# A two-layer trunk with four token mixers and a mixture of experts: the first layer's experts in groups of four with 96 slots each, norm1 without GpSimd, rows replicated on the host, and another instruction order

## The chip, the cores and the metric

One NeuronCore of a Trainium2 chip runs the whole program; the other cores are idle. The metric is device time in microseconds of one execution. The profile names the engines PE (TensorE matmul), PEld (TensorE weight load), DVE (VectorE), ACT (ScalarE), POOL (GpSimd) and SP (SyncE, which here only issues DMAs); PEclk is the granted TensorE clock as a share of the higher of its two levels (1.2 and 2.4 GHz).

## The reference, cut to what matters

```python
D_MODEL, SEQ, DEPTH, CTX_LEN = 1024, 256, 2, 256
N_EXPERTS, TOP_K, D_EXPERT = 16, 2, 256
def adaln(cond, w_mod, b_mod):
    m = jax.nn.silu(cond) @ w_mod + b_mod          # w_mod 1024 x 6144
    return jnp.split(m[..., None, :], N_MOD, axis=-1)
def trunk_layer(x, xc, ...):
    h = rms_norm(x, lp["norm1_g"]) * (1.0 + mod[1]) + mod[0]      # latent; hc for context likewise
    ... = jnp.split(h @ lp["w_in"], splits, axis=-1)              # w_in 1024 x 6544
    ya_l, yb_l, yc_l, yd_l = fourier, RWKV-7, DeltaNet, S5 mixers
    x = x + mod[2] * merge_branches((ya_l, yb_l, yc_l, yd_l), gate_l, lp["w_branch"], lp["w_out"])
    h2 = rms_norm(x, lp["norm2_g"]) * (1.0 + mod[4]) + mod[3]
    x = x + mod[5] * moe_ffn(h2, ...)
def moe_ffn(h, ...):                                # two experts of one group of four per token
    for e in range(N_EXPERTS):
        act = jax.nn.silu(h @ w1[e]) * (h @ w3[e])  # 1024 -> 256
        y = y + combine[..., e:e + 1] * (act @ w2[e])
```

Layer 0 computes 512 tokens (256 of context, 256 latent) and layer 1 needs only the 256 latent ones at its end. All is float32.

## The kernel before, in words

**Recording and order.** The kernel doesn't issue its instructions as it goes. Every operation is recorded, cut into some 1,480 units, and `nc.plan(RUNS)` goes over them: RUNS, a table of numbers, is the order of priority, and a cost model decides for each engine which ready operation comes next and which buffer it gets (43 buffers of 128 x 1024 words for weights, tokens and results, 8 PSUM banks). The program then holds one fixed order for each engine. SP issues most of the loads, ACT the small ones and the experts' result writes, POOL the gathers. A load takes one of eight semaphores in turn, shared by the loads of SP and of ACT, so an issue can wait for the load that had its semaphore before.

**Layer start.** `adaln` (before: matmul L1917, after: L1945) multiplies the two condition rows by w_mod, in rounds of 16 tiles `aw` of 512 KB; a matmul has 32 columns of weights, and four of them stand side by side in the array. `norm1_cols` (L1949) transposes the shift and scale of round 0. `norm1` (L1985) transposes the tokens with a diagonal matrix that holds 1/rms, and evicts each chunk of 128 x 256 as a high part `hT` (ACT, L1991) and a low part `hTl` (DVE L1992, then a subtraction at L1993 that alternates between DVE and POOL), so that the float32 input projection (`gemm`, L763) can run as products of two cheaper floats. The weights `cw` are split likewise (L639, L640).

**Mixers.** `s5_setup` builds the S5 branch's matrices from its parameters by many small matmuls (L1582 and L1606 to L1613) with DVE, ACT and POOL work between them. It doesn't depend on the tokens.

**Experts.** `moe` routes the tokens, writes them to DRAM (`h2d`), and takes the experts as blocks. In layer 0 a block is one expert with 128 slots: a gather of 128 token rows (`xg`), 8 transposes (L2115), 8 matmuls of 128 columns by 512 for w1 and w3 (`expert_up`, L2127), the activation (L2132 to L2134), 2 transposes (L2144), 4 matmuls by w2 (`expert_down`, L2154), and a write of the block's rows to DRAM (`ybd`). Each expert has 6 weight tiles `w` of 512 KB (L2092, L2096). Then each token gathers its two rows back (`yg`) and they are added with their weights (L2448 to L2450). In layer 1 a block is two experts with 64 slots, side by side in the array. A block of code under `tc.If(most > cap)` (L2401 to L2409) computes every expert for every token if an expert has more tokens than slots; with these inputs the largest expert has 96 tokens in layer 0 and 52 in layer 1.

```python
o1, ne = s5_setup(k, 1), NEXP + 2            # layer 1's S5 set-up is recorded among layer 0's experts
```

Of the kernel before, what the change touches and what calls it, by code (L numbers as in the profile page):

```python
# [24 lines left out]
NJ = 8  # L25
# [9 lines left out]
def host_consts():  # L35
# [18 lines left out]
    for k in c:  # L54
# [14 lines left out]
PACK = PRM + [("c", 16), ("norm1_g", 8), ("norm2_g", 8), ("s5_lam", 32), ("s5_log_step", 16), ("dn_ab", 16),  # L69
              ("router_w", 128), ("router_b", 16)]  # L70
# [6 lines left out]
def host_layout(a):  # L77
# [4 lines left out]
    for L in range(2):  # L82
# [3 lines left out]
        for n in ("norm1_g", "norm2_g"):  # L86
            p[n] = a[n][L].reshape(8, 128).T
# [110 lines left out]
def cost(o):  # L198
# [4 lines left out]
    if "dma" in o.name:  # L203
        return (0, 440, 0, 1000, 375)[o.eng], 0, math.prod(out.shape) * 4
    if o.eng == 0:
        if o.name == "transpose":
            return int(.85 * max(size(o.args[1]), size(o.args[2]))), 210, 0
        m, n = size(o.kw["lhsT"]), size(o.kw["rhs"])
        if o.kw["rhs"].dtype == F32:
            d = 2 * max(.85 * m + 4, .85 * n)  # L210
        else:
            d = max(.85 * m, .45 * n + 8)
        return int(d), 210, 0
    n = max([size(x) for a in list(o.args) + list(o.kw.values()) for x in aps(a)])
    if o.eng == 1:
        return int(50 + .9 * n), 160, 0
# [13 lines left out]
def part(o):  # L230
# [5 lines left out]
    n = len(rs) * len(cs)  # L236
    return sum(1 << (4 * x + y) for x in rs for y in cs), 100 if n > 8 else 50 if n > 4 else 35
# [27 lines left out]
class Tape:  # L265
    def __init__(self, tc, wk, ps):
# [6 lines left out]
        self.ops, self.tiles, self.spans, self.state, self.last_pe = [], {}, {}, {}, {}  # L273
# [17 lines left out]
    def access(self, ap):  # L291

        key = ap.tensor.name
        if key in self.tiles or ap.space != bass.MemoryType.DRAM:
            width = self.tiles[key].ap.shape[1] if key in self.tiles else NFIX
            c = (key in self.tiles, width, ap.offset, tuple(map(tuple, ap.ap)), ap.dtype)
# [8 lines left out]
    def add(self, eng, name, args, kw, reads=None, writes=None):  # L305
# [17 lines left out]
        for x, wr in [(r, False) for r in reads] + [(w, True) for w in writes]:  # L323
# [21 lines left out]
            else:  # L345
                st[1].append((op.pos, r0, r1, m))
            if eng == 0 and wr:
                o = self.last_pe.get(key)
                if o is not None:
                    op.pre.setdefault(o, 0)  # L350
                self.last_pe[key] = op.pos
# [11 lines left out]
    def plan(self, order=None):  # L363
# [23 lines left out]
        tiles.sort(key=lambda v: v.first)  # L387

# [25 lines left out]
        front, tab, wire, clock = 0, 0, 0, Clock()  # L414
        free, port = [0] * 6, [0] * 6
# [4 lines left out]
        for count in range(n):  # L420
# [30 lines left out]
            for v in new:  # L451
# [4 lines left out]
                if v.first > front:  # L456
                    held[v.kind][front:v.first] += 1
            d, f = o.dur, table(o)
            if f >= 0 and f != tab:
# [13 lines left out]
            if o.nbytes:  # L473
                wire = max(wire, t + d + 1300) + o.nbytes // 300
                o.end = wire + 500
# [320 lines left out]
def load_params(k, L):  # L796
# [3 lines left out]
    m = NPK - (144 if L else 0)  # L800
# [41 lines left out]
def rwkv(k, L, want_ctx):  # L842
# [180 lines left out]
    for s in range(8):  # L1023
# [69 lines left out]
    nc.scalar.dma_start(ln[:, 0], k.A["rw_ln_g"][L][None, :].to_broadcast([128, 256]))  # L1093
    nc.scalar.dma_start(ln[:, 1], k.A["rw_ln_b"][L][None, :].to_broadcast([128, 256]))
# [38 lines left out]
def deltanet(k, L, want_ctx):  # L1133
# [217 lines left out]
    for g in range(4):  # L1351
        p = psum(k, "dd")
        for u in range(8):
            for d in range(2):
                R = rows(d)
                nc.tensor.matmul(p[rows(1 - d), u * 64:u * 64 + 64], lhsT=KG[g // 2][R, g % 2 * 8 + u], rhs=ATu[R, g * 8 + u],
                                 start=True, stop=True, tile_position=(64 * d, 64 - 64 * d))
        for d in range(2):
            O = rows(1 - d)
            (nc.vector.tensor_copy if d else nc.scalar.copy)(hp2(WT[d][g // 2])[O, g % 2 * 512:g % 2 * 512 + 512], p[O])  # L1360
# [403 lines left out]
def fnet(k, L, want_ctx):  # L1764
# [808 lines left out]
```

## Time and profile before

| | us |
|---|---|
| time, median of 3 runs | 1659.14 (1657.5 to 1659.85) |
| time of the profiled execution | 1656.07 |
| its span | 1654.3 |
| PE busy in it | 1463.3 (88%) |
| PEld, DVE, ACT, POOL busy | 1031.0, 1054.4, 496.2, 359.1 |

The profiled execution lies 3.1 us under the median, and its time is 1.8 us longer than its span. Shares of the whole span hide that the stages have different limits, so the program is read here by stages: start 0 to 97 us (modulation, norm1), mixers and merge of layer 0 97 to 701, routing 701 to 768, experts of layer 0 768 to 983, combine and norm1 of layer 1 983 to 1033, mixers and merge of layer 1 1033 to 1490, routing 1490 to 1530, experts of layer 1 1530 to 1630, end 1630 to 1654.

### The profile page before, as it was taken

What the parts mean: (1) busy time and instruction counts of PE and PEld (TensorE: products, weight loads), DVE (VectorE), ACT (ScalarE), POOL (GpSimd) and SP (SyncE); (2) the same over time, 40 slices, a digit from 0 to 9 for tenths busy, and PEclk for the clock granted to TensorE, in tenths of its full rate; (3) what the DMA queues carried; (4) which work ended last, traced back from release to release, by engine and by line L of the source; (5) the groups of instructions that cost most, each with busy time, mean ns of one, the idle gap of its engine ahead of it and who ended that gap; (6) DMA issues with size and microseconds to landing.
All of it is one profiled execution on the core that took longest, in us unless ns stands there. A gap on an engine that the chain in (4) does not pass through costs nothing. (4 is left out here: it accounts for less than half of the span.)

```text
span 1654.3 us, 26410 instructions
## 1 busy us (share of the span) xinstructions
PE 1463.3 (88%) x10334; PEld 1031.0 (62%) x10334; DVE 1054.4 (64%) x2224; ACT 496.2 (30%) x826; POOL 359.1 (22%) x352
## 2 busy tenths in 40 slices
PE   3799999999999997976999987999999999687993
PEld 0477778778668774754444444877877778576430
DVE  7763993787795677776211234598996977766213
ACT  2224344343223333001111122246542344421100
POOL 5300420000311255412000243222003012341000
PEclk8679999999999999956999997899898999896997
DMA  8303042212571475384978764330235763892994
GB/s 333 133 22 82 10 147 86 77 61 78 206 270 48 153 290 234 124 354 131 345 279 306 282 230 151 91 115 7 103 94 182 284 224 121 301 362 107 388 361 181
DMA packets 106505, 304.01 MB, mean 184 GB/s; under 512 B 14440, under 2 KB 28904, under 8 KB 106376
## 3 DMA queue, kind: packets, MB, share of 16 engines
q1 hardware_dynamic: 84976, 255.05, 42.9%
q10 hardware_dynamic: 16792, 30.45, 5.7%
q0 software_dynamic: 4608, 16.78, 2.8%
q8 instruction: 83, 1.36, 0.3%
q14 instruction: 46, 0.38, 0.1%
HBM read 270.22 MB, written 32.01 MB: 183 GB/s over the span
## 5 line engine op out<-in xcount | busy, mean ns | idle before, releaser
L763 PE MATMUL gemm<-hT,cwh 128*128 128x512 f32 (+1 forms) x1648 | 466.6, 365 | 8.6 <-DVE cwh L640 4.2
L763 PEld LDWEIGHTS gemm<-hT,cwh 128*128 128x128 f32 x1648 | 300.0, 197 | 72.5 <-issue 13.2
L763 PE MATMUL gemm<-hTl,cwh 128*128 128x512 f32 (+1 forms) x824 | 295.1, 359 | 0.5 <-DVE hTl L1993 0.5
L640 DVE TENSOR_TENSOR cwh<-cw,cwh 128x1024 fp32r<-128x1024 f32 x118 | 151.0, 1281 | 93.5 <-PE gemm L763 40.9
L639 ACT CAST cwh<-cw 128x1024 fp32r<-128x1024 f32 x118 | 123.0, 1047 | 192.6 <-PE gemm L763 87.3
L2127 PE MATMUL rr<-w,xgT 128*128 128x512 f32 (+1 forms) x512 | 176.8, 595 | 2.4 <-DMA w<-in_moe_w_dram 2.3
L763 PEld LDWEIGHTS gemm<-hTl,cwh 128*128 128x128 f32 x824 | 162.5, 197 | 24.6 <-issue 3.7
L2127 PEld LDWEIGHTS rr<-w,xgT 128*128 128x128 f32 (+1 forms) x512 | 65.6, 163 | 93.1 <-issue 82.0
L2133 DVE SCALAR_TENSOR_TENSOR act<-act,rr 128x256 f32<-128x256 f32 x24 | 10.1, 420 | 135.3 <-ACT act L2132 135.3
L1917 PE MATMUL ada<-aw,fixed 128*32 128x512 f32 x384 | 72.9, 704 | 24.5 <-DMA aw<-in_w_mod_dram 24.5
L2154 PE MATMUL gemm<-w,act 128*128 128x512 f32 (+1 forms) x256 | 90.7, 599 | 3.3 <-ACT act L2145 2.2
L2034 PE MATMUL gate<-yh,cwh 128*128 128x512 f32 (+1 forms) x384 | 83.0, 360 | 3.1 <-ACT yh L639 1.5
L2081 PE MATMUL gemm<-wouth,mTh 128*128 128x512 f32 x288 | 69.9, 400 | 7.1 <-DVE wouth L640 5.9
L2034 PEld LDWEIGHTS gate<-yh,cwh 128*128 128x128 f32 x384 | 61.0, 198 | 17.8 <-issue 4.2
L2081 PEld LDWEIGHTS gemm<-wouth,mTh 128*128 128x128 f32 x288 | 54.5, 192 | 21.7 <-DVE wouth L640 7.6
L2037 POOL TENSOR_TENSOR mT<-mT,th 128x512 f32<-128x512 f32 (+1 forms) x48 | 57.2, 1213 | 41.7 <-DVE th L2035 32.3
L2154 PEld LDWEIGHTS gemm<-w,act 128*128 128x128 f32 (+1 forms) x256 | 32.7, 163 | 47.7 <-issue 35.2
L2132 ACT ACTIVATE act<-rr 128x256 f32<-128x256 f32 x24 | 9.2, 384 | 150.8 <-PE rr L2127 127.7
L1985 PE MATMUL dd<-diag,x 128*128 128x128 f32 x128 | 33.2, 427 | 19.6 <-ACT hT L1991 12.0
L2007 ACT ACTIVATE gth<-gemm 128x512 f32<-128x512 f32 (+1 forms) x64 | 30.8, 488 | 50.3 <-PE gemm L763 31.5
L2436 POOL DMA_INDIRECT yg<-ybd,fixed x12 | 11.4, 951 | 154.4 <-DMA ybd<-yo 140.4
L1985 PEld LDWEIGHTS dd<-diag,x 128*128 128x128 f32 x128 | 27.5, 310 | 26.1 <-ACT hT L1991 15.4
(510 smaller groups left out, 2578.5 us busy)
## 6 DMA issues: line engine op xcount, KB each, us to landing
w<-in_moe_w_dram SPq DMA_DIRECT2D x192, 512.0 KB
cw<-in_w_tile_dram SPq DMA_DIRECT2D x102, 512.0 KB
aw<-in_w_mod_dram SPq DMA_DIRECT2D x96, 512.0 KB
th<-thd SPq DMA_DIRECT2D x24, 512.0 KB
ybd<-yo ACTq DMA_DIRECT2D x24, 512.0 KB
thd<-gth SPq DMA_DIRECT2D x16, 512.0 KB
cw<-in_w_branch_dram SPq DMA_DIRECT2D x16, 512.0 KB
wout<-in_w_out_dram SPq DMA_DIRECT2D x16, 512.0 KB
```

The source lines that it names most:

```text
L639: k.nc.scalar.copy(hi, raw)
L640: k.nc.vector.tensor_tensor(lo, raw, hi.bitcast(F32), op=OP.subtract)
L763: mm3(k, p[:, lo:hi], sub(w, ALL, j), sub(k.hT[j], ALL, slice(lo, hi)), j == 0, j == NJ - 1, skip_group_check=lo > 0)
L1917: nc.tensor.matmul(p[q:q + 32], lhsT=k.cs[:, j].rearrange("p s n -> p (s n)"), rhs=ws[m][:, h * 512:h * 512 + 512], start=(j == 0), stop=( ...
L1985: nc.tensor.matmul(p[:, o:o + 128], lhsT=xs[tt][:, (j2 * 2 + jj) * 128:(j2 * 2 + jj) * 128 + 128], rhs=diag[:, tt], start=True, stop=True)
L2007: nc.scalar.activation(th[:, n % 2], p[:, lo:], AF.Tanh, scale=0.5)
L2034: mm3(k, p[:, :N], sub(wb, ALL, t, slice(n % 4 * 128, n % 4 * 128 + 128)), sub(y, ALL, t), t == 0, t == 1)
L2037: nc.gpsimd.tensor_tensor(acc, acc, t_, op=OP.add)
L2081: mm3(k, p, sub(mT[n // per], ALL, n % per, tk), sub(wo[n], ALL, cs), n == 0, n == 7)
L2127: nc.tensor.matmul(ph[M], lhsT=xT[j][:, M], rhs=w13[j], start=(j == 0), stop=(j == NJ - 1), tile_position=(0, i * C), skip_group_check=True)
L2154: nc.tensor.matmul(p[M], lhsT=aT[:, t, M], rhs=w2[t][:, cs], start=(t == 0), stop=(t == 1), tile_position=(0, i * C), skip_group_check=True)
L2436: nc.gpsimd.indirect_dma_start(out=g, out_offset=None, in_=ybd, in_offset=bass.IndirectOffsetOnAxis(ap=sl[:, x, n:n + 1], axis=0))
```

## The change

**Experts of layer 0.** An expert has 96 slots. Four experts make a group with three blocks of 128 rows: the first 64 slots of experts 0 and 1, the first 64 of experts 2 and 3, and 32 more slots of each of the four. So 16 blocks become 12, the matmuls of a block are two of 64 columns or four of 32 side by side, and a group's three `up` products are recorded together before the `down` of the group before. The slot of a token and the one-hot for the gather are worked out for the new layout (two more iotas, twice two one-hot comparisons for each of four token tiles, some 20 small DVE operations). The fallback's limit becomes 96.

**norm1.** ACT writes the high part and then `rest = high - shift`; DVE makes the low part from the PSUM chunk in one operation. POOL has no part in it.

**Rows.** The adaLN bias, norm2_g, the RWKV norm rows and final_g come replicated over partitions from the host and are read by plain loads, where broadcast reads of DRAM were used.

**Order.** The planner counts the time of a load otherwise, treats a PSUM tile as one piece and has other costs; two PSUM tiles are split in two; RUNS holds another order.

```diff
 def norm1(k, xs, s, sc, sh):
+    nsh = keep(k, "nsh", [128, 2, NJ])[:, s]
+    nc.vector.tensor_scalar(nsh, sh[:, s], -1.0, None, op0=OP.mult)
...
-            nc.scalar.activation(hi, i, AF.Identity, scale=sc[:, s, j:j + 1], bias=sh[:, s, j:j + 1])
-            nc.vector.tensor_scalar(raw, i, sc[:, s, j:j + 1], sh[:, s, j:j + 1], op0=OP.mult, op1=OP.add)
-            (nc.gpsimd if j % 2 else nc.vector).tensor_tensor(lw, raw, hi.bitcast(F32), op=OP.subtract)
+            nc.scalar.activation(hi, p[:, jj * 256:jj * 256 + 256], AF.Identity, scale=sc[:, s, j:j + 1], bias=sh[:, s, j:j + 1])
...
+            nc.scalar.activation(rest[:, jj], hi.bitcast(F32), AF.Identity, bias=nsh[:, j:j + 1])
...
+            nc.vector.scalar_tensor_tensor(lw, p[:, jj * 256:jj * 256 + 256], sc[:, s, j:j + 1], rest[:, jj], op0=OP.mult,
+                                           op1=OP.subtract)
...
+FOUR = ((0, 1), (2, 3), (0, 1, 2, 3))
...
+    def group(g):
+        xT = [rows_in(3 * g + b) for b in range(3)]
+        w13s, w2s = zip(*[k.pre.pop(e, None) or expert_weights(k, L, e) for e in range(4 * g, 4 * g + 4)])
+        ph = [psum(k, "rr") for _ in range(3)]
+        for j in range(NJ):
+            for p, x, n, es in zip(ph, xT, (64, 64, 32), FOUR):
+                for i, e in enumerate(es):
+                    M = slice(i * n, i * n + n)
+                    nc.tensor.matmul(p[M], lhsT=x[j][:, M], rhs=w13s[e][j], start=(j == 0), stop=(j == NJ - 1),
+                                     tile_position=(0, i * n), skip_group_check=True)
+        return [(expert_act(k, p), [w2s[e] for e in es]) for p, es in zip(ph, FOUR)]
...
+    def group_down(g, ups):
+        for b, (act, w2) in enumerate(ups):
+            yo = expert_down(k, act, w2, (64, 64, 32)[b])
+            nc.scalar.dma_start(ybd[(3 * g + b) * 128:(3 * g + b) * 128 + 128], yo)
...
-        b = A["b_mod"][L, c0:c0 + 2 * D].rearrange("(m h n) -> h m n", m=2, h=2)
-        for h in range(2):
-            nc.scalar.dma_start(bm[rows(h)], b[h][:, None, :].to_broadcast([2, 32, 512]))
+        nc.scalar.dma_start(bm, A["ada_rows"][L, r])
...
-            o.end = wire + 500
+            lanes[e == 3].append(o.end)
...
-        ffn = moe(k, L, project_out(k, L, lo, src, md[L], tiles, xs), xs, md[L], tiles, 128 if want else 64, 128 if want else 64)
+        ffn = moe(k, L, project_out(k, L, lo, src, md[L], tiles, xs), xs, md[L], tiles, 96 if want else 64, 96 if want else 64)
...
-    1, 29, 30, 2, 10, 0, 37, 11, 12, 13, 14, 15, 16, 17, 18, 34, 35, 36, 44, 42, 38, 39, 40, 41, 43, 65, 53, 45, 66,
+    2, 10, 11, 13, 12, 37, 14, 15, 97, 3, 84, 16, 17, 18, 34, 4, 35, 5, 6, 0, 42, 19, 20, 7, 60, 24, 8, 36, 21, 103,
```

The first place is the start of SP's program, before: `cw` are projection weights, `kc` and `prm` constants and parameters, `s5m` the S5 parameters, `aw` the tiles of w_mod.

```order
L750 DMA cw<-in_w_tile_dram 128x1024
L802 DMA fixed<-in_prm_dram 128x303
L583 DMA fixed<-in_kc_dram 128x976
L1545 DMA s5m<-in_prm_dram 128x1024
L802 DMA fixed<-in_prm_dram 128x159
L1913 DMA aw<-in_w_mod_dram 128x1024 x10
```

The same place after the change:

```order
L832 DMA fixed<-in_prm_dram 128x295
L1941 DMA aw<-in_w_mod_dram 128x1024 x10
L1949 DMA x_174<-in_ctx_dram 128x1024
L1949 DMA x_189<-in_ctx_dram 128x1024
L1941 DMA aw<-in_w_mod_dram 128x1024 x2
L1949 DMA x_237<-in_x_dram 128x1024
L1949 DMA x_254<-in_x_dram 128x1024
L1941 DMA aw<-in_w_mod_dram 128x1024 x3
L613 DMA fixed<-in_kc_dram 128x976
L1574 DMA s5m<-in_prm_dram 128x1024
L1941 DMA aw<-in_w_mod_dram 128x1024
L780 DMA cw<-in_w_tile_dram 128x1024 x14
```

Fifteen of the sixteen `aw` tiles stand ahead of `kc`, `s5m` and every `cw`; the last parameters (128 x 135 columns now) went behind the first 14 `cw`. On PE the first rows of before are:

```order
L1917 MATMUL ada<-aw,fixed 32x512 x17
L1608 MATMUL ss<-s5m 16x16
L1917 MATMUL ada<-aw,fixed 32x512 x3
L1606 MATMUL ss<-s5V,s5m 16x112
L1608 MATMUL ss<-s5m 16x16
L1609 MATMUL ss<-s5bb,s5m 16x16
```

After the change (`dd` is norm1's product, L2015):

```order
L1945 MATMUL ada<-aw,fixed 32x512 x28
L2015 MATMUL dd<-diag,x_174 128x128
L2015 MATMUL dd<-diag,x_189 128x128
L2015 MATMUL dd<-diag,x_174 128x128
L2015 MATMUL dd<-diag,x_189 128x128
L1945 MATMUL ada<-aw,fixed 32x512 x4
```

No S5 matmul stands ahead of PE's first `gemm` in the new program (24 further `dd` and the 8 of `norm1_cols` lie between); S5 set-up begins behind it, among the projections. The second place is PE among layer 0's experts, before:

```order
L2127 MATMUL rr<-w_5865,xgT 128x512 x2
L2127 MATMUL rr<-w_5868,xgT 128x512 x2
L2127 MATMUL rr<-w_5872,xgT 128x512 x2
L2127 MATMUL rr<-w_5875,xgT 128x512 x2
L2127 MATMUL rr<-w_5891,xgT 128x512 x2
```

and after, where each `w` is another expert's tile:

```order
L2448 MATMUL rr<-w_6197,xgT 64x512
L2448 MATMUL rr<-w_6406,xgT 64x512
L2448 MATMUL rr<-w_6436,xgT 64x512
L2448 MATMUL rr<-w_6525,xgT 64x512
L2448 MATMUL rr<-w_6197,xgT 32x512
L2448 MATMUL rr<-w_6406,xgT 32x512
L2448 MATMUL rr<-w_6436,xgT 32x512
L2448 MATMUL rr<-w_6525,xgT 32x512
L2187 MATMUL dd<-fixed,act 128x128 x2
```

Pairs of 64 columns and fours of 32 stand in place of whole-width matmuls, and four weight tiles are in use at a time. Column width changes between neighbouring matmuls 101 times in the stage, 48 times before. The third place is PE at the end of layer 0's experts, before (L1606 is S5 set-up of layer 1):

```order
L2144 MATMUL dd<-fixed,act 128x128 x2
L1606 MATMUL ss<-s5V,s5m 16x112 x6
L2154 MATMUL gemm<-w_6975,act 128x512
L2144 MATMUL dd<-fixed,act 128x128 x2
L2154 MATMUL gemm<-w_6992,act 128x512
```

and the last expert matmuls after the change, with what follows them:

```order
L2197 MATMUL gemm<-w_6937,act 64x512
L2197 MATMUL gemm<-w_7013,act 64x512
L2197 MATMUL gemm<-w_6986,act 64x512
L2197 MATMUL gemm<-w_7016,act 64x512
L1638 MATMUL ss<-s5bb,s5m 16x16
L1639 MATMUL ss<-fixed,s5bb 16x16
L1642 MATMUL ss<-s5V,s5m 16x112 x2
L1637 MATMUL ss<-s5m 16x16
```

Most of layer 1's S5 set-up now stands behind the last expert matmul, ahead of the combine, and not between the experts.

## Rows read from the trace of the kernel before

**Rows 1.** Windows by stage: us, busy PE PEld DVE ACT POOL (instructions), PEclk, DMA share, GB/s.
```profile
0.00:64.00 64.00, 30.29 (x178) 11.30 (x179) 55.55 (x146) 16.56 (x29) 33.86 (x34) 0.81 0.79 301
64.00:97.00 33.00, 27.07 (x160) 20.21 (x161) 13.19 (x36) 10.96 (x20) 5.80 (x7) 0.50 0.06 18
97.00:647.00 550.00, 530.38 (x4147) 400.75 (x4146) 397.94 (x725) 198.06 (x309) 112.78 (x111) 0.97 0.38 131
...
701.00:768.00 67.00, 42.08 (x252) 32.14 (x251) 57.20 (x270) 8.88 (x21) 10.92 (x17) 0.56 0.63 245
768.00:983.00 215.00, 210.48 (x795) 101.83 (x794) 47.63 (x84) 36.79 (x76) 39.16 (x24) 0.99 0.80 289
983.00:1033.00 50.00, 31.68 (x106) 19.71 (x105) 21.00 (x49) 16.40 (x29) 19.86 (x19) 0.73 0.52 163
...
1530.00:1630.00 100.00, 93.37 (x433) 35.17 (x429) 19.79 (x35) 8.02 (x19) 0.00 (x0) 1.00 0.91 348
```

**Rows 2.** Waits of SP's queue, 0 to 70 us: total, times, longest.
```profile
SPq L1913 <- DMA abm<-in_b_mod_dram: 8.3, 2, 4.2
```

**Rows 3.** Timeline of SP, 0 to 70 us: start, length, issues.
```profile
10.21 9.96 SPq L1913 DMA_DIRECT2D aw<-in_w_mod_dram  x10
```

**Rows 4.** Windows of 10 us, columns as in rows 1.
```profile
10.00:20.00 10.00, 0.85 (x5) 0.23 (x8) 6.88 (x41) 1.68 (x4) 2.18 (x2) 1.00 0.68 235
30.00:40.00 10.00, 6.74 (x38) 1.70 (x37) 9.97 (x8) 4.60 (x8) 7.69 (x4) 0.50 1.03 409
```

**Rows 5.** Timeline of PE, 0 to 97 us: start, length, work, [idle before].
```profile
19.15 1.94 PE L1917 MATMUL ada<-aw,fixed 128*32 128x512 f32 x8 [19.15 <-DMA aw<-in_w_mod_dram]
...
53.27 1.04 PE L1917 MATMUL ada<-aw,fixed 128*32 128x512 f32 x2
...
63.82 1.61 PE L1985 MATMUL dd<-diag,x 128*128 128x128 f32 x6 [0.81 <-issue]
...
96.42 0.80 PE L763 MATMUL gemm<-hT,cwh 128*128 128x512 f32 x1
```

**Rows 6.** Groups by line and shape: busy us, mean ns, idle before and its releasers.
```profile
L1991 ACT ACTIVATE hT<-dd,fixed 128x256 fp32r<-128x256 f32 x32 | 17.9, 564 | 41.6 <-PE dd L1985 29.7 <-DVE hraw L1992 6.0 <-DVE s5E L1480 3.9
L2132 ACT ACTIVATE act<-rr 128x256 f32<-128x256 f32 x24 | 9.2, 384 | 150.8 <-PE rr L2127 127.7 <-DMA ybd<-yo 16.6 <-DMA fg<-in_final_g_dram 6.5
L639 ACT CAST cwh<-cw 128x1024 fp32r<-128x1024 f32 x118 | 123.0, 1047 | 192.6 <-PE gemm L763 87.3 <-DVE cwh L640 32.9 <-PE ada L1917 14.2
```

**Rows 7.** Timeline of PE: a merge at 643 us, layer 0's experts, layer 1's experts.
```profile
643.32 1.06 PE L1917 MATMUL ada<-aw,fixed 128*32 128x512 f32 x8
644.32 1.89 PE L2034 MATMUL gate<-yh,cwh 128*128 128x512 f32 x7
...
794.05 3.60 PE L2154 MATMUL gemm<-w,act 128*128 128x512 f32 x8
...
798.77 7.03 PE L2127 MATMUL rr<-w,xgT 128*128 128x512 f32 x16
...
822.30 1.09 PE L2115 MATMUL dd<-fixed,xg 128*128 128x128 f32 x8 [0.68 <-ACT xgT L2116]
...
1533.48 9.65 PE L2127 MATMUL rr<-w,xgT 128*64 128x512 f32 x42
```

**Rows 8.** Timeline of PE, end of layer 0's experts to layer 1's first projection.
```profile
957.29 0.55 PE L1606 MATMUL ss<-s5V,s5m 64*16 64x112 f32 x4
...
962.36 1.95 PE L1949 MATMUL ada<-fixed,abm 128*128 128x4 f32 x16
...
968.28 7.16 PE L2127 MATMUL rr<-w,xgT 128*128 128x512 f32 x16
...
984.61 0.55 PE L1582 MATMUL ss<-fixed,s5Wh 128*128 128x128 f32 x3
991.29 16.34 PE L2448 MATMUL dd<-yg,dw 128*128 128x512 f32 x32 [6.14 <-DMA yg<-ybd,fixed]
...
1032.81 0.56 PE L763 MATMUL gemm<-hT,cwh 128*128 128x256 f32 x1
```

More of the change, by code (lines that the diff above doesn't have):

```diff
@@ L235, in part @@
     rs, cs = range(r // 32, (r + w.shape[0] - 1) // 32 + 1), range(c // 32, (c + size(w) - 1) // 32 + 1)
[L236 to L237 removed]
+    n, m = len(rs) * len(cs), size(o.args[1] if o.name == "transpose" else o.kw["rhs"])
+    f = 100 if n > 8 else 65 if n > 4 else 90 if n < 4 else 35 if m > 255 else 62
+    if 4 < n < 9 and m > 255:
+        f = 50
+    return sum(1 << (4 * x + y) for x in rs for y in cs), f
 def table(o):
@@ L345, in add @@
             else:
+                if key in self.tiles and self.tiles[key].kind == "q":
+                    for o in st[1]:
+                        if o[0] < op.pos and self.ops[o[0]].eng != eng:
+                            op.pre.setdefault(o[0], 0)
                 st[1].append((op.pos, r0, r1, m))
[L347 to L351, printed above, removed]
         for key in op.uses:
@@ L387, in plan @@
         tiles.sort(key=lambda v: v.first)
+        users = {}
+        for o in ops:
+            for x in o.uses:
+                users.setdefault(x, []).append(where[o.pos])
         small = []
@@ L1351, in deltanet @@
     for g in range(4):
-        p = psum(k, "dd")
+        ps = [psum(k, "dd") for _ in range(2)]
         for u in range(8):
@@ L2371, in down @@
         nc.scalar.dma_start(ybd[bl * 128:bl * 128 + 128], yo)
-    prev, xT = None, rows_in(0)
-    dw = None
+    def group(g):
[13 more added lines that the diff above has]
+            nc.scalar.dma_start(ybd[(3 * g + b) * 128:(3 * g + b) * 128 + 128], yo)
+    dw = None
+    if not few:
+        ups = None
+        for g in range(4):
+            cur = group(g)
+            if ups:
+                group_down(g - 1, ups)
+            ups = cur
+            if g == 1:
+                dw = t4(k, [128, 4, 2, 128], "dw")
+                for n in range(NT):
+                    for x in range(2):
+                        nc.scalar.activation(dw[:, n, x], k.ident, AF.Copy, scale=wk[:, 2 + x, n:n + 1])
+            yield
+        group_down(3, ups)
+        nblk = 0
+    prev, xT = None, rows_in(0) if few else None
     for bl in range(nblk):
@@ L2381, in moe @@
         prev = cur
-        if not few and bl == 4:
-            dw = t4(k, [128, 4, 2, 128], "dw")
-            for n in range(NT):
-                for x in range(2):
-                    nc.scalar.activation(dw[:, n, x], k.ident, AF.Copy, scale=wk[:, 2 + x, n:n + 1])
         yield
-    down(nblk - 1, *prev)
+    if few:
+        down(nblk - 1, *prev)
     yield
```

124 lines of the change are left out of this document (84 added, 40 removed), and 139 rows, old and new, of the table RUNS.

## The prediction

> **What bounds the kernel now.** I read the windows by stage first [rows 1], since the share of busy time over the whole span (PE 88%) mixes stages with different limits. Three kinds of stage are to be seen. In the mixers of layer 0 (97 to 647 us) PE works 530 of 550 us at a granted clock of 0.97, and among layer 0's experts (768 to 983 us) 210.5 of 215 us at 0.99: there PE sets the pace and only less PE work shortens the stage. The start is different: up to 64 us PE is busy 30 us, and from 64 to 97 us it is at the lower clock (0.50) while the DMA queues carry 18 GB/s. Between 983 and 1033 us PE works 32 of 50 us.
>
> Then the start in detail. SP waits 8.3 us in two pieces for the bias rows `abm` [rows 2], because a new load has to wait for the load that used its semaphore before, and the bias rows are broadcast reads that land late. So the ten first `aw` issues begin at 10.21 us [rows 3]. From 10 to 20 us the queues carry 235 GB/s, and 409 when they are full [rows 4]. PE's first modulation matmul starts at 19.15 us, the last of the sixteen tiles' matmuls end at 54.3 us (53.27 + 1.04), norm1 begins at 63.82 us and the first projection at 96.42 us [rows 5]. From 54.3 us to 96.4 us hardly anything is loaded, and S5 set-up and norm1 take turns on PE, ACT, DVE and POOL.
>
> **The start, term by term.** After the change one parameter load stands ahead of the first `aw` on SP and one plain 256 KB load is the bias, so I let the first `aw` start at 2 us instead of 10.21. Ahead of the last `aw` stand 16 `aw`, 4 token tiles, `kc`, `s5m` and parameters, some 22 tiles of 0.524 MB, 11.7 MB. At 409 GB/s they take 28.6 us. A tile lands some time after its issue; from 10.21 to the first matmul at 19.15 us it was 8.9 us at worst, and I take 4. The modulation then ends near 35 us (2 + 28.6 + 4); at the mean rate of the start, 301 GB/s [rows 1], it would be 45 us. The columns for norm1 cost 4 us (2 to 9.5, which is the gap from 54.3 to 63.82 us, with S5 work in it).
>
> norm1's chunks are then paced by ACT. Of 32 chunks the new order has 28 transposed ahead of the first projection, in 14 evictions. Each costs one high part (0.564 us) and one `rest`, which the trace doesn't show: the nearest ACT operations of that size are the 0.384 us of the experts' activation and again 0.564 [rows 6], and I take 0.47. That is 14 x 1.03 = 14.5 us, with four weight casts of 1.05 us between them 18.7, and I take 19. First projection at 35 + 4 + 19 = 58 us: **-38** (bounds 54 and 75 us: -42 and -21). What POOL no longer does (its subtraction at L1993) lies beside this path and is counted at nothing; if ACT's second pass were not hidden behind matmul and DVE it is already in the 19.
>
> What was done meanwhile has to be done elsewhere. The S5 set-up of layer 1, which does the same work, shows its size at full clock [rows 8]: from 957.29 to 968.28 us, less the 1.95 us of norm1's columns, 9.0 us, and from 975.4 us (968.28 + 7.16) to 985.2 us, less one `down` of 3.60 [rows 7], 6.1 us: 15 us. For layer 0 most of it, I take 13, moves into the mixers, where PE has nearly no idle time: **+13** (0 if it fills the 20 idle us, 20 if its DVE chains also hold PE up). Start together: **-25**.
>
> **The experts of layer 0.** One fp32 matmul is two records. Eight whole-width `up` matmuls take 7.03 us, 0.88 each; four `down` 3.60 us, 0.90 each [rows 7]. So 16 blocks cost 16 x (7.03 + 3.60) = 170 us. After, a block of two halves has its price in layer 1, 42 records in 9.65 us, 10.5 pairs of 0.92 us. A four of 32 columns has its price in the modulation: 8 records between 643.32 us and the next matmul at 644.32, 1.00 us [rows 7]. With 12 matmul sets for each of 12 blocks there are 48 triples of two pairs and one four, 48 x (2 x 0.92 + 1.00) = 136.3 us: **-33.7**. Four blocks fewer save four times the 8 token transposes (1.09 us) and the two of the activation, together **-5.5**. About 12 of the 15 us of S5 set-up no longer stand between the experts, some 2 still do: **-10**.
>
> Against this stands the load. The stage carries 215 us x 289 GB/s = 62 MB now; four gathers and four writes of 0.524 MB go, 58 MB stay. PE's work falls to about 166 us (215 - 33.7 - 5.5 - 10), and 58 MB in 166 us are 349 GB/s, what the experts of layer 1 get at a DMA share of 0.91 (348) [rows 1]. The margin of before (0.80) is used up, so waits for weights must be expected; a group also holds 24 of the 43 buffers. I take **+9** (0 if the 409 GB/s of the start are to be had, 35 if 289 GB/s remain the rate). Stage together: -40, 215 to 175 us.
>
> One sentence of the Trainium skill speaks against this part, TensorEngine Tiling (Array Packing), section Key Properties: changing the tiling mode drains the TensorE. The new order changes it 101 times, the old one 48 times. The burst of 32 columns between whole-width matmuls, 1.00 us against 0.88 [rows 7], has two such changes in it, so the trace shows little of a drain, at most 0.06 us a change, 3 us for 53 more changes; by its full length of 1.06 us it would be 0.18 each and 10 us. The four is already priced at 1.00, so the sum keeps the first.
>
> **Routing.** It is DVE's stage (57 of 67 us) [rows 1]. Comparisons over 16 x 96 in place of 16 x 128 slots cover a quarter fewer elements but are eight instructions for four. Some 20 small operations are added: at the stage's mean of 0.21 us (57.2 / 270) they are 4 us, but they make the slots that only the gather back needs, so the experts hide them. I take **0** (-2 to +4).
>
> **Combine and norm1 of layer 1.** S5 set-up stands behind the last `down` now. PE idles 6.14 us ahead of the combine, for the block's write and the gather, with little set-up left [rows 8]; some 10 us of set-up now fill that wait and overrun it by **+3** (0 to 6). The first projection stands behind 12 norm1 products, 27 before, which with the wait ahead of them fill the 25 us between the combine's end (1007.6) and 1032.81: I take **-5** (0 to -10), since the other products come later at ACT's pace.
>
> **Sum.** -25 - 40 + 3 - 5 = -67. From the profiled time of 1656.07 that is 1589; the median of the runs lies 3.1 us above that execution, so I predict 1592 us. The stages that I count at nothing, both mixers, are ordered anew too; PE's idle time in layer 0's (20 us) [rows 1] bounds a gain there, and I give +-10 for both.
>
> **The rivals.**
> (a) *Weights set the pace of the experts.* For it: 58 MB at the present 289 GB/s take 201 us, and four tiles of different experts must be there for one set. Against it: 348 GB/s in layer 1's experts. Then the stage loses only 14 us and the time is 1618.
> (b) *The start's gain is eaten in the mixers.* DVE works 55.6 of the first 64 us, much of it on S5; put into the mixers (DVE 398 of 550) it can leave the S5 branch late, and PE waits there for what it saved. Then only experts and combine gain, 42 us: 1617.
> (c) *The other side: each group waits for its weights.* A group's 24 tiles are 12.6 MB, 43.6 us at 289 GB/s; if their buffers come free only with the group before, only its `down` products, 12 sets of about 0.95 us, 11.4 us, hide them. Then 32 us stand open at each of three groups, 96 us in place of the 9: 1679, slower. It decides from 26 us a group upward. Against it: a tile is given back after its own six or so matmuls, and the order has most tiles used several matmul sets after their buffer is free.
> (d) *Nothing comes of it*: the largest expert has just 96 tokens, and one more would send every expert through the fallback; or gains and stalls cancel: 1659.
>
> **Numbers.** Forecast 0.72, (a) 0.11, (b) 0.09, (c) 0.05, (d) 0.03. The measurement can tell about 0.2%, 3.3 us. (a) and (b) are still faster, so faster 0.91, same 0.03, slower 0.06. The low end takes the good bounds together in part (no waits -9, start -4, mixers -10, norm1 -5: 1564, with some room 1560); the high end holds (a) and (b) with 14 us for both being mixed with a slow start: 1632. The forecast's own range is 1565 to 1612.
>
> **What would show it.** Right: first projection near 58 us; the mixers' stage some 13 us longer in PE busy time; 64-column pairs near 0.92 and fours near 1.00 us; the expert stage near 175 us at over 320 GB/s with single waits of PE for `w` adding to under 10 us; PE busy among the experts near 166 us. Wrong: PE waits for `w` of 20 us at the start of a group (c) or spread over the stage with the DMA share at 0.9 (a); PE idle in the mixers over 35 us with S5 as the releaser (b); fours at 1.3 us and more, since then the third block costs what it saves.

## The result and the profile after

The changed kernel takes 1674.22 us (median of 6 runs, 1665.89 to 1679.95), the kernel before, on the same chip, 1658.32 us (6 runs). The ratio is 1.0102 [1.0059, 1.0146]: slower by 1%, clear of the noise, where I had forecast 1592 us and a gain. The profiled execution of the changed kernel took 1665.89 us, 9.8 more than that of before. It is the fastest of the six, 8.3 us under their median, so the stages below add up to 9.5 us and not to the 15.9 between the medians.

The first view to read is again the windows by stage, columns as in [rows 1], with the stages moved to where they now lie: start, mixers of layer 0, merge and routing, experts, mixers of layer 1, experts of layer 1.

```profile
0.00:52.10 52.10, 26.93 (x135) 13.19 (x136) 34.78 (x141) 23.22 (x43) 19.30 (x29) 0.71 0.95 374
...
52.00:711.00 659.00, 582.38 (x4349) 447.27 (x4349) 433.59 (x759) 213.47 (x338) 123.57 (x118) 0.90 0.32 108
711.00:811.00 100.00, 83.75 (x400) 63.47 (x398) 69.87 (x312) 10.82 (x20) 34.65 (x32) 0.77 0.67 247
811.00:992.00 181.00, 167.45 (x970) 52.09 (x972) 62.72 (x115) 27.91 (x59) 38.44 (x20) 0.97 0.82 306
...
1029.00:1475.00 446.00, 401.80 (x3863) 335.08 (x3861) 363.52 (x646) 190.88 (x321) 94.22 (x107) 0.92 0.43 143
1529.00:1639.00 110.00, 103.17 (x499) 43.43 (x500) 21.31 (x39) 9.35 (x23) 0.00 (x0) 0.97 0.90 349
```

To compare the kernels I mark the same events in both on PE's timeline and take the differences:

| stretch, from event to event | before us | after us | change | forecast |
|---|---|---|---|---|
| start, to the first projection | 96.4 | 52.1 | -44.3 | -38 |
| mixers of layer 0, to `project_out` | 551.0 | 659.6 | **+108.6** | **+13** |
| `project_out` and routing | 120.2 | 99.5 | -20.7 | 0 |
| experts of layer 0 | 214.4 | 181.1 | -33.3 | -40 |
| last `down` to the combine | 9.3 | 15.2 | +5.9 | +3 |
| combine to layer 1's first projection | 41.5 | 21.5 | -20.0 | with the next, -5 |
| mixers of layer 1 | 429.8 | 446.1 | +16.3 | |
| the rest of layer 1 | 188.0 | 185.1 | -2.9 | 0 |
| sum | 1650.6 | 1660.1 | +9.5 | -67 |

Each stretch that the change was costed for came out within 7 us of its forecast, or better. One stage, at which I had looked for 13 us, lost 109 and took all of it. The windows of that stage say what kind of loss it is: PE busy 582 us in 659 against 530 in 550 [rows 1], so 52 us more busy time and 57 us more idle time, at a granted clock of 0.90 in place of 0.97.

Where in the stage it happens is seen when it is cut at one event: the first DVE transposition of the RWKV branch's triangular inverse. Windows of the kernel before, up to that event and behind it, then two 20 us windows behind it:

```profile
97.00:338.00 241.00, 231.73 (x1244) 180.62 (x1243) 166.71 (x266) 100.05 (x153) 38.34 (x29) 0.97 0.23 72
338.00:647.00 309.00, 298.65 (x2905) 220.13 (x2904) 231.23 (x460) 98.01 (x156) 74.44 (x83) 0.98 0.50 178
...
380.00:400.00 20.00, 19.89 (x306) 15.32 (x305) 13.31 (x8) 8.12 (x13) 0.00 (x0) 1.00 0.33 107
400.00:420.00 20.00, 20.00 (x384) 17.26 (x385) 13.77 (x26) 7.19 (x16) 3.51 (x7) 1.00 0.01 3
```

The same windows of the changed kernel, and four of 20 us:

```profile
52.00:373.00 321.00, 300.13 (x1773) 234.20 (x1773) 204.49 (x312) 127.84 (x206) 49.95 (x37) 0.97 0.22 68
373.00:712.00 339.00, 283.25 (x2582) 213.89 (x2581) 229.48 (x449) 85.70 (x132) 74.62 (x82) 0.83 0.42 146
...
380.00:400.00 20.00, 3.61 (x40) 3.17 (x40) 18.84 (x43) 1.06 (x1) 2.36 (x1) 0.58 0.00 1
400.00:420.00 20.00, 5.02 (x94) 4.91 (x94) 19.04 (x32) 1.13 (x2) 0.00 (x0) 0.50 0.00 0
420.00:440.00 20.00, 19.52 (x267) 17.53 (x268) 7.56 (x11) 5.29 (x12) 3.09 (x4) 0.50 0.01 2
...
540.00:560.00 20.00, 20.00 (x261) 19.40 (x262) 4.80 (x9) 7.67 (x11) 5.81 (x5) 0.50 0.06 15
```

Ahead of the inverse PE now does 68 us more (300.1 against 231.7), so the inverse starts 321 us after the first projection and not 241. Behind it PE is busy 15 us less (283.3 against 298.7, now at a clock of 0.83 and not 0.98) and the stretch still takes 30 us more (339 against 309). Of PE's windows, taken for the projections' line alone (us, busy PE, PEld), the first kernel here is the one before:

```profile
97.00:337.60 240.60, 178.86 (x726) 137.57 (x725) 0.97 0.23 71
337.60:647.00 309.40, 128.09 (x499) 92.09 (x497) 0.98 0.50 178
```

and this the changed one:

```profile
52.00:372.90 320.90, 217.37 (x877) 167.25 (x878) 0.97 0.22 68
372.90:711.70 338.80, 98.20 (x348) 66.76 (x346) 0.83 0.42 146
```

151 of 1,225 projection matmuls went from behind the inverse to ahead of it (877 less 726, and 499 less 348), 38.5 us (217.4 less 178.9). Matmuls of the tile `ss` add 18.2 us there (49.6 against 31.4): about 7 are the Fourier mixer's, which uses that tile too, and 11 are S5's. DeltaNet's make up most of the remaining 12. What the projections covered before lies bare now. DVE's timeline of the changed kernel shows the serial chain (62 small operations of L736 and L738 in turn, of which the first and the last stand here, then the transpositions that PE waits for):

```profile
372.87 7.85 DVE L728 STREAM_TRANSPOSE rriA<-AT 32x1024 f32<-32x1024 f32 x4
...
381.21 0.21 DVE L736 TENSOR_TENSOR rriT<-rriA,rriX 128x31 f32<-128x31 f32 x1
...
408.84 0.19 DVE L738 TENSOR_TENSOR rriX<-rriX,rriT 128x31 f32<-128x31 f32 x1
409.07 3.80 DVE L750 STREAM_TRANSPOSE AT<-rriX 32x1024 f32<-32x1024 f32 x2
412.88 1.93 DVE L756 STREAM_TRANSPOSE rriT<-rriX 32x1024 f32<-32x1024 f32 x1
```

and PE's timeline of the same kernel shows that the last projection ends at 376.9 us, ahead of the 62 operations, and that only small matmuls of DeltaNet are left for PE under the chain:

```profile
376.50 0.40 PE L793 MATMUL gemm<-hT,cwh 128*128 128x512 f32 x1
...
385.23 0.69 PE L1282 MATMUL dd<-fixed 128*64 128x64 f32 x6
414.95 2.74 PE L764 MATMUL rr<-rriT,AT 32*32 32x32 f32 x48 [29.04 <-DVE rriT L756]
```

The projections are not used up: 98.2 us of them still stand behind the inverse. But SP issues one `cw` tile at 329.73 us and the next ones at 452.94, so hardly any of their weights are loaded in the meantime.

### The profile page after: what moved, and what is told of

It reads as the page before. It is cut to its first block, busy times and chain, and to the rows that moved or that the text cites. A ratio compares the mean times of both kernels' runs of the same rounds, so it can differ in the third digit from the quotient of the medians.

```text
span 1664.1 us, 26932 instructions
## 1 busy us (share of the span) xinstructions
PE 1441.9 (87%) x10662; PEld 1011.0 (61%) x10662; DVE 1050.8 (63%) x2220; ACT 498.2 (30%) x842; POOL 347.0 (21%) x334
## 5 line engine op out<-in xcount | busy, mean ns | idle before, releaser
L793 PE MATMUL gemm<-hT,cwh 128*128 128x512 f32 (+1 forms) x1648 | 468.4, 367 | 33.3 <-ACT cwh L669 12.9
L793 PE MATMUL gemm<-hTl,cwh 128*128 128x512 f32 (+1 forms) x824 | 300.6, 366 | 0.7 <-DVE hTl L2026 0.7
L2448 PE MATMUL rr<-w,xgT 128*32 128x512 f32 (+1 forms) x512 | 97.9, 609 | 4.2 <-DVE xgT L2150 3.5
L2068 PE MATMUL gate<-yh,cwh 128*128 128x512 f32 (+1 forms) x384 | 77.6, 354 | 6.7 <-DVE th L2069 5.1
L2197 PE MATMUL gemm<-w,act 128*64 128x512 f32 (+1 forms) x384 | 79.5, 599 | 2.3 <-DVE yo L2202 1.9
L2161 PE MATMUL rr<-w,xgT 128*64 128x512 f32 x256 | 61.0, 607 | 7.2 <-DMA w<-in_moe_w_dram 6.7
L2448 PEld LDWEIGHTS rr<-w,xgT 128*32 128x32 f32 (+1 forms) x512 | 21.5, 123 | 74.3 <-issue 64.4
L2197 PEld LDWEIGHTS gemm<-w,act 128*64 128x64 f32 (+1 forms) x384 | 23.0, 127 | 47.0 <-issue 35.2
L1047 POOL COPY SU<-VV 64x256 f32<-64x256 f32 x32 | 17.7, 561 | 152.8 <-PE rr L1085 135.6
L1185 DVE SCALAR_TENSOR_TENSOR dnu<-gemm,fixed,dnu 128x508 f32<-128x508 f32 (+3 forms) x48 | 33.1, 697 | 23.1 <-ACT dnu L1177 22.6
```

What stands on the lines that cost most here:

```text
L793: mm3(k, p[:, lo:hi], sub(w, ALL, j), sub(k.hT[j], ALL, slice(lo, hi)), j == 0, j == NJ - 1, skip_group_check=lo > 0)
L1185: nc.vector.scalar_tensor_tensor(oo, ii, cv[:, tap:tap + 1], oo, op0=OP.mult, op1=OP.add)
L2068: mm3(k, p[:, :N], sub(wb, ALL, t, slice(n % 4 * 128, n % 4 * 128 + 128)), sub(y, ALL, t), t == 0, t == 1)
L2161: nc.tensor.matmul(ph[M], lhsT=xT[j][:, M], rhs=w13[j], start=(j == 0), stop=(j == NJ - 1), tile_position=(0, i * C), skip_group_check=True)
L2197: nc.tensor.matmul(p[M], lhsT=aT[:, t, M], rhs=w2[t][:, cs], start=(t == 0), stop=(t == 1), tile_position=(0, i * C), skip_group_check=True)
L2448: nc.tensor.matmul(p[M], lhsT=x[j][:, M], rhs=w13s[e][j], start=(j == 0), stop=(j == NJ - 1), tile_position=(0, i * n), skip_group_check=True)
```

## The experiments

**Theory A** (order): the new order moves the work that covered RWKV's serial chain ahead of it, and the loss is the bare chain with what follows it at the lower clock. **Rival B**, (b) of the prediction: the S5 set-up put into the mixers eats the start's gain. **Rival C**: the new code (norm1, start, groups of four) costs it, whatever the order. **Rival D**: the idle wait alone lowers the clock behind it.

**Order of before, S5 late alone, S5 first.** All have the new code. In the first the units of start and layer 0's mixers stand in the order of before; the second is the first with `s5_setup(k, 0)` behind the first projections; the third is the changed kernel's order with `s5_setup(k, 0)` ahead of everything.

```diff
-        pS = [psum(k, "rr") for _ in range(2)]
+        pS = [psum(k, "rr") for _ in range(2)] if L else [psum(k, "rr")] * 2
...
-        ps = [psum(k, "dd") for _ in range(2)]
+        ps = [psum(k, "dd") for _ in range(2)] if L else [psum(k, "dd")] * 2
...
-    2, 10, 11, 13, 12, 37, 14, 15, 97, 3, 84, 16, 17, 18, 34, 4, 35, 5, 6, 0, 42, 19, 20, 7, 60, 24, 8, 36, 21, 103,
+    1, 29, 30, 2, 10, 0, 37, 11, 12, 13, 14, 15, 16, 17, 18, 34, 35, 36, 44, 42, 38, 39, 40, 41, 43, 65, 53, 45, 66,
```

> All of the change but the order of the start and of layer 0's mixers, where the units stand as before the change (S5 set-up at the start too); the two PSUM tiles that were split are one again in layer 0. Theory A (the new order does other PE work ahead of RWKV's serial DVE inverse, PE runs dry in it and goes on at the lower clock): first projection near 96 us, mixers near 551 us instead of 659, time near 1605 us. Rival B (the S5 set-up that moved into the mixers costs it there): the same here. Rival C (the new code of the mixers or the planner's PSUM rule is what is slow): mixers stay over 620 us, time near 1700 us.

> As the first kernel, but S5 set-up's units are moved back behind the first projections, so that the start is short as after the change and everything else in layer 0's mixers keeps the old order. Theory A: first projection near 56 us, mixers some 575 us (551 and about 22 of S5 work), time near 1585 us. Rival B: mixers over 630 us, time near 1650 us.

> The changed kernel with one move: S5 set-up of layer 0 stands ahead of everything, the rest of the new order is kept. Theory A: first projection near 97 us, mixers still 635 to 645 us, time near 1695 us. Rival B: mixers near 560 us, time near 1615 us.

| | start | mixers of layer 0 | time us (runs) | ratio to before |
|---|---|---|---|---|
| after | 52.1 | 659.6 | 1674.22 (6) | 1.0102 [1.0059, 1.0146] |
| order of before | 97.1 | 585.3 | 1680.58 (8) | 1.0104 [1.0057, 1.0151] |
| the same, S5 late | 58.3 | 607.1 | 1651.07 (7) | 0.9928 [0.9896, 0.996] |
| changed order, S5 first | 97.2 | 627.7 | 1698.77 (2) | 1.0212 [1.0129, 1.0295] |

My times for the first two were missed. I expected 1605 and 1585 us and they took 1680.58 and 1651.07; their mixers took 585 and 607 us and not 551 and 575. Layer 1's mixers also take 470.9 and 458.3 us in them, 446.1 in the changed kernel, though their order numbers are the same; why was not told apart. The third kernel came out near what theory A said (627.7 for 635 to 645 us, 1698.77 for 1695).

The four make a square. Moving S5 alone takes 39 to 45 us from the start and puts 22 (in the order of before) or 32 (in the new one) into the mixers: dearer than my 13, but a gain of 13 to 17 us each time, so B is not the cause. The order of the rest, at one place for S5, is worth 53 us (659.6 against 607.1) or 42 (627.7 against 585.3). Together the two moves are 74 of the 109 us (659.6 against 585.3). With S5 first the wait at the inverse is still there, in the waits of that kernel (engine, tile, line, what it waits for, total us, times, longest):

```profile
PE rr L764 <- DVE rriT L756: 28.2, 1, 28.2
```

The order of before with the new code comes to 585 us, though, and not to 551: these 34 us are there with numbers that were made for the old code. PE waits more for the splits of the projection weights, in the waits of that kernel (before, 1.6 us for DVE's):

```profile
PE gemm L793 <- DVE cwh L670: 9.2, 5, 6.6
PE gemm L793 <- ACT cwh L669: 5.2, 3, 4.0
```

The rest of the 34 us was not told apart.

**Dense matmuls in the wait.** The changed order, with 28 dense matmuls that nobody reads put ahead of the inverse's products:

```diff
+        for _ in range(fill if hf == 0 else 0):
+            nc.tensor.matmul(p1[0], lhsT=k.ident, rhs=XF, start=True, stop=True)
```

> The changed kernel with 28 extra matmuls of 128x512 float32 on TensorE that feed nothing, in the place where PE waits for RWKV's inverse (about 25 us of work inside a 29 us wait). The rest of the program keeps its order. If the lower clock after the wait costs what I read from the windows (380 to 480 us), PE's clock stays at 1.0 there and the time falls by 10 to 20 us, to about 1650; if the clock after the wait doesn't matter, the time is the same within 3 us; if the extra matmuls delay something, it is longer.

1673.99 us (8 runs), ratio 1.0081 [1.0043, 1.0119], mixers 656.5 us: no change beyond 3 us. Its 20 us windows:

```profile
380.00:400.00 20.00, 19.20 (x45) 8.66 (x46) 18.84 (x43) 1.06 (x1) 2.37 (x1) 1.00 0.00 1
...
420.00:440.00 20.00, 19.43 (x267) 17.57 (x268) 7.54 (x11) 5.53 (x11) 3.36 (x4) 0.50 0.01 2
```

The clock holds at 1.00 while the dense matmuls run, and from 420 to 440 us it is 0.50 as without them. But the filling doesn't reach the end of the wait. PE is through with it, and with the DeltaNet matmuls behind it, at 407.4 us, and 7.42 us of the wait are left, in PE's timeline of that kernel:

```profile
414.86 2.76 PE L769 MATMUL rr<-rriT,AT 32*32 32x32 f32 x48 [7.42 <-DVE rriT L759]
```

The clock falls in this rest, ahead of the first product, while PE is idle:

```profile
408.00:410.00 2.00, 0.00 (x0) 0.00 (x0) 1.84 (x5) 0.00 (x0) 0.00 (x0) 1.00 0.00 0
411.00:414.00 3.00, 0.00 (x0) 0.00 (x0) 2.99 (x2) 0.00 (x0) 0.00 (x0) 0.50 0.00 0
```

So this run doesn't take the idle time away. It decides neither on rival D nor on what the lower clock costs, and the expectation of the next run is wrong to take the wait as filled.

**Wide matmuls between the narrow ones.** As before with 24, and one wide matmul of 256 columns after every fourth step of the two loops of 32x32 products:

```diff
+            if fill and u % 4 == 3:
+                nc.tensor.matmul(p3[:, 0:256], lhsT=k.ident, rhs=XD, start=True, stop=True)
```

> The changed kernel with matmuls that feed nothing: 24 of 128x512 in the wait for RWKV's inverse, as before, and 16 of 128x256, whole width, spread between the 128 matmuls of 32x32 that follow it (415 to 445 us). Their added work also moves the order of later layers a little, so only that stretch is read. If it is the narrow matmuls alone that let the granted clock fall (they fill TensorE's time but it stood at 0.50 from 420 to 440 us even when the wait ahead was filled), the clock there is over 0.7 with the wide ones between. If the clock falls for another reason, it is 0.50 as before.

1691.26 us (one run), mixers 679.5. My expectation of a clock over 0.7 was missed from 420 to 440 us, as the 10 us windows say:

```profile
420.00:430.00 10.00, 10.00 (x62) 6.59 (x62) 0.00 (x0) 0.58 (x1) 0.00 (x0) 0.50 0.01 2
430.00:440.00 10.00, 10.00 (x80) 6.90 (x78) 1.28 (x3) 2.08 (x5) 0.79 (x2) 0.50 0.00 0
440.00:450.00 10.00, 10.00 (x185) 8.32 (x184) 2.90 (x7) 2.95 (x7) 0.79 (x2) 0.81 0.01 3
```

The wide matmuls were not few: from 420 to 440 us they take 11.4 of PE's 20 us (7.00 and 4.36 in windows of their two lines, L774 and L783). Here too PE was idle just ahead, 6.69 us up to 413.74, and from 410 to 420 us the clock is 0.50 already. So this run doesn't show that the narrow matmuls alone let it fall.

**New code, order improved.** The new code with one planner cost set back, the share of the array that a matmul counts for, and the numbers of "S5 late alone", those behind layer 0's mixers too, improved by a search under that cost:

```diff
-    f = 100 if n > 8 else 65 if n > 4 else 90 if n < 4 else 35 if m > 255 else 62
-    if 4 < n < 9 and m > 255:
-        f = 50
-    return sum(1 << (4 * x + y) for x in rs for y in cs), f
+    return sum(1 << (4 * x + y) for x in rs for y in cs), 100 if n > 8 else 50 if n > 4 else 35
```

> All of the change with another order: the start and layer 0's mixers from the second kernel (old order, S5 set-up late), then searched again with one cost of the planner set back, the share by which a narrow matmul counts as activity for the clock (0.35 and 0.50 of a whole one, where the change has 0.35 to 0.90); the two split PSUM tiles are one again in layer 0. Theory A (only the order lost the time; experts, norm1 and the short start are gains): first projection near 50 us, mixers near 585 us, experts as short as after the change (some 200 us from first transpose to combine), layer 1 no longer than before, time near 1605 us, faster than both. Rival C (the new code costs it, whatever the order): not under 1645 us.

**1614.15 us** (4 runs, 1610.5 to 1620.0), ratio 0.9739 [0.9694, 0.9784]: it beats both kernels, by 45 and by 60 us. Its windows up to the inverse, behind it, and 20 us of the inverse's products:

```profile
50.00:334.00 284.00, 254.87 (x1447) 195.99 (x1447) 208.90 (x321) 110.67 (x174) 67.32 (x42) 0.93 0.21 61
334.00:640.00 306.00, 297.03 (x2895) 219.32 (x2895) 236.13 (x460) 101.38 (x161) 74.13 (x81) 0.98 0.52 181
...
380.00:400.00 20.00, 20.00 (x387) 16.17 (x386) 10.68 (x11) 6.99 (x13) 0.79 (x2) 1.00 0.28 96
```

and PE's timeline there, where projections (L790) lie between the 32x32 products (L761, L768):

```profile
385.55 0.39 PE L790 MATMUL gemm<-hT,cwh 128*128 128x512 f32 x1
385.87 1.32 PE L761 MATMUL rr<-rriT,AT 32*32 32x32 f32 x36
387.12 0.50 PE L790 MATMUL gemm<-hT,cwh 128*128 128x512 f32 x1
387.45 0.40 PE L790 MATMUL gemm<-hTl,cwh 128*128 128x512 f32 x1
387.69 0.39 PE L790 MATMUL gemm<-hT,cwh 128*128 128x512 f32 x1
```

Behind the inverse this kernel is back at 297 us busy of 306, at 0.98, as before. Rival C falls as a cause of the loss: the new code, start, norm1 and groups of four, is part of the fastest kernel here. I had expected some 1605 us, and one part of that was missed: layer 1's mixers are 452.7 us against 429.8 before. Against this kernel the changed one's mixers have 70 us more (659.6 less 589.8): 38.5 of it idle (659.6 - 583.0 and 589.8 - 551.7) and 31 more busy time of PE on the same work.

**Planner of before; the share alone; the same code searched.** The first is the order of before with all of the old planner (load times, costs, one PSUM tile). The second is the changed kernel with only the share of above set back and its own numbers. The third is the second with the numbers searched from the changed kernel's.

```diff
-                s = t + d + 1300
...
-                lanes[e == 3].append(o.end)
+                wire = max(wire, t + d + 1300) + o.nbytes // 300
+                o.end = wire + 500
```

> As the first kernel (old order in the start and layer 0's mixers, all else of the change kept), and with the planner's costs and rules of before as well. What follows layer 0's mixers was searched for the other planner and will be poor, so only the start and the mixers are read, by the profile. If the 34 us by which the first kernel's mixers (585 us) are longer than before (551) come from the planner's new costs under the same order numbers: mixers 545 to 560 us. If they come from the new code (norm1, rows, constants), mixers near 585 us.

> The changed kernel with the same order numbers and one cost of the planner set back: the share by which a narrow matmul counts as activity for the clock. If that cost misplaces the work directly, layer 0's mixers fall from 660 to under 635 us and the time to about 1645; if the order numbers decide, mixers stay at 650 to 670 us and the time near 1672.

> The changed kernel, its code untouched, with that one cost set back and its order numbers improved by the same kind of search for a while, starting from the numbers of the change. Theory A (only the order lost the time): mixers near 625 us, time near 1640 us. Rival C (new code of the mixers): over 1660 us.

| | start | mixers of layer 0 | time us (runs) | ratio to before |
|---|---|---|---|---|
| old planner | 84.2 | 583.0 | 1703.8 (1) | |
| share alone | 51.7 | 659.6 | 1666.12 (8) | 1.0044 [1.0007, 1.0082] |
| same code, searched | 53.5 | 634.1 | 1646.61 (5) | 0.9938 [0.9888, 0.9987] |

The old planner missed my 545 to 560 us: start and mixers together are 667 us, 20 over those of before (647), for the new code with numbers made for the old. That is not explained here. The share alone leaves the mixers as they were, so the table of numbers holds the loss, not this cost at work on it. A search takes 25 us from the mixers, near what I had expected, and yet the wait stays, in its waits of layer 0:

```profile
PE rr L761 <- DVE rriT L753: 33.0, 2, 32.6
```

**The inverse's chain left out.** The changed order with 61 of the DVE operations of the first inverse skipped; everything else stands as it was. What it leaves out is the triangular solve, so the tokens go to other experts, one has more than 96, and the fallback runs; only the mixers of layer 0 are read.

```diff
+                    if o.pos in self.skip:
+                        n += 1
+                        continue
```

> The changed kernel without 61 of the 62 DVE operations of RWKV's first inverse in layer 0 (its forward substitution), so that the output isn't the reference's; every other instruction stands where it stood. Theory A (TensorE has nothing left to do in that chain): the 29 us wait nearly goes, layer 0's mixers fall by 24 to 28 us to about 633, the time to about 1647. If other DVE work or the scan behind it is late anyway, the mixers fall by under 10 us.

The whole takes 2962.19 us (2 runs), of which some 1,310 are the fallback: 1,324.9 us from the last `down` to the combine, where the changed kernel has 15.2. The mixers are 628.2 us, 31.4 less. The wait is nearly gone, in the waits from 330 to 440 us:

```profile
PE rr L769 <- DVE rriT L761: 5.1, 2, 4.6
```

So the bare chain is worth some 30 of the 109 us, measured by itself, and no more: 24.4 are the wait (29.5 less 5.1), and the other 7 were not told apart. Behind the shortened wait the clock is 0.50 all the same (390 to 410 us), so it isn't the 29 us of idle time that the lower clock needs; shorter ones stand ahead here, 3.26, 1.06 and 4.56 us.

## Why the prediction was wrong

**The step that failed** is the one with which I closed the sum: "The stages that I count at nothing, both mixers, are ordered anew too; PE's idle time in layer 0's (20 us) [rows 1] bounds a gain there, and I give +-10 for both." It bounds a gain and says nothing of a loss. I had looked at the order at its start, among the experts and at their end, where the diff spoke, and not at what lies under RWKV's chain, where nothing in the diff points. The +13 for S5 was a busy time at the full clock, and moving S5 cost 22 to 32 us. The projections that moved ahead of the inverse took with them cover that I counted on without looking.

What stands in its place, of +108.6:
- 21 us are busy time that the improved order has too: 551.7 us there, 530.4 before. About 17 of it are matmuls of the tile `ss`, so of S5 (54.3 against 37.5). I had 13 for it.
- 31 us are more busy time on the same work than in the improved order (583.0 - 551.7), in stretches such as 420 to 440 and 540 to 560 us at 0.50. Added up over windows of 1 us, PE is busy 98 us at the lower level in the changed kernel's mixers, 35 in the improved order's and 28 before. The 32x32 products take about twice as long there (48 in 2.74 us at 0.50, 85 in 2.20 us at 1.00 in the kernel before). If all work does, the 64 us between 98 and 35 hold 32 us of loss. That is an estimate; no run took the clock alone away.
- some 30 us are the bare chain (29.0 in the waits, 31.4 when it is left out);
- the remaining 27 of the 57 us of idle time are smaller waits, not told apart. The largest is 6.5 us, of the projections for a result of ACT (`gth`).

The sign that I had set for rival (b) was over 35 us of PE idle with S5 as the releaser. PE idles 77 us here, but its waits for S5's operands come to 1 us, this one the longest:

```profile
PE ss L1637 <- DVE ss L1630: 0.7, 1, 0.7
```

So (b) is not what happened. In the improved order such waits are some 10 us (4.6, 2.9 and shorter ones).

Why the search that made the new numbers took this order was not shown. The changed share is a suspect, but only two searches under the old one speak for it.

**The start**: forecast -38, measured -44.3. In SP's timeline of the changed kernel:

```profile
1.20 6.20 SPq L1941 DMA_DIRECT2D aw<-in_w_mod_dram  x10
```

and in PE's of the same kernel:

```profile
7.19 1.93 PE L1945 MATMUL ada<-aw,fixed 128*32 128x512 f32 x8 [7.19 <-DMA aw<-in_w_mod_dram]
...
37.43 1.95 PE L1977 MATMUL ada<-fixed,abm 128*128 128x4 f32 x16 [0.25 <-DVE abm L1952]
...
52.14 0.47 PE L793 MATMUL gemm<-hT,cwh 128*128 128x512 f32 x1
```

The first `aw` is issued at 1.20 us (I had 2), the columns come at 37.4 (35), and norm1 needs 12.8 us from their end to the first projection where I had 19. The unseen `rest` is 0.511 us against my 0.47, by form in the changed kernel:

```profile
L2023 ACT ACTIVATE hraw<-hT,fixed 128x256 f32<-128x256 f32 x32 | 14.4, 511 | 1.3 <-DVE fixed L2008 1.3
```

**The experts**: forecast 175, measured 181. PE is busy 167.5 us there (forecast near 166). The load is no bound: no wait for `w` stands among PE's, at 306 GB/s and a share of 0.82, so rivals (a) and (c) are out and my +9 had the wrong cause: PE idles 13.5 us, for other reasons. What PE waits for is the gather of the tokens, the largest of that stage's waits:

```profile
PE dd L2149 <- DMA xg<-h2d,fixed: 6.0, 3, 2.8
```

The price of two pairs and a four is read where a whole group's `up` runs in one piece (a row merges shapes and bears the first one's):

```profile
817.94 24.02 PE L2448 MATMUL rr<-w,xgT 128*64 128x512 f32 x128
```

128 records are 8 triples, 3.00 us each, and I had 2.84. With two changes of width in a triple the difference is 0.08 us a change, part of it the lower clock at its start (0.76 from 811 to 830 us). I had set two sums beside the Trainium skill's sentence on the drain (TensorEngine Tiling (Array Packing), section Key Properties), and the second was wrong: 1.06 less 0.88 us stands for two changes, so it is 0.09 us a change and not 0.18. The 0.08 lies between 0.06 and 0.09.

**Routing**: forecast 0, measured -20.7 with `project_out`. I had priced the new small operations and overlooked what leaves: the DVE work of layer 1's S5 set-up stood in that stretch before. DVE is busy 69.9 us there now against 98.6 in 647 to 768 us before. No run tested this cause, and a gain that I hadn't forecast is luck.

**Combine and layer 1**: +5.9 for +3, and -20.0 + 16.3 = -3.7 for -5. The gain ahead of the first projection comes back behind it, as forecast. That the sum came within 2 us is partly luck: layer 1's mixers lie at 442 to 471 us in the variants with the new code (478 with the old planner), and why was not told apart.

With +13 for the mixers the stages would add up to -86 us. The gains of the start and of the experts hold; the order that came with them does not.

## What to carry to other kernels

A change that orders the work anew has to be read where the longest serial chain of another engine runs: list what PE does under it before and after, and price it as bare if that work has moved ahead. A stage without idle time bounds what can be gained there, never what can be lost. An order made for a kernel should be tried apart from its code: here nearly the same code (one planner cost and two split PSUM tiles apart) was 45 us faster than before with one order and 16 us slower with another.

## What the runs showed of the hardware

TensorE was granted 0.50, the lower of its two levels (1.2 GHz), while it was busy 19.5 of 20 us (420 to 440 in the changed kernel) and 20.0 of 20 us (540 to 560), but for the last 0.2 us of the first stretch with matmuls that move at most 64 columns. So busy time alone didn't bring the higher level back.

The clock came down in two ways. Ahead of RWKV's products it fell while TensorE idled, in the changed kernel and in both kernels with added matmuls. The other fall lies between 536 and 537 us of the changed kernel: TensorE had been busy without a gap since 533.82 with 32x32 products, behind a wait of 1.18 us. PE's timeline and a window of the changed kernel show it (from 540 us the clock is 0.50):

```profile
533.82 2.08 PE L764 MATMUL dd<-ddiT,AT 32*32 32x32 f32 x61 [1.18 <-DVE ddiT L756]
```

```profile
534.00:536.00 2.00, 2.00 (x73) 2.00 (x70) 1.99 (x2) 0.58 (x1) 0.00 (x0) 1.00 0.03 8
```

So rival D can hold for the first place, and it isn't all there is to the second. Small matmuls don't always bring the clock down either. In the improved order they ran alone for 8.6 us at 1.00, behind projections and without a gap:

```profile
388.10:396.70 8.60, 8.60 (x242) 7.79 (x242) 1.75 (x4) 3.84 (x8) 0.79 (x2) 1.00 0.20 74
```

What decides between the two was not settled here. In the run with 256-column matmuls between the narrow ones, the clock was down before the first product and still 0.50 from 430 to 440 us. So small matmuls can cost more than the wait ahead of them: where the clock was down, 19.5 us of work in 20 didn't raise it.
